# Differential attention's score products: three products of the halves, the third over 64 rows of the array

## The chip, the core and the metric

The kernel runs on one core of a Trainium2 chip. A core has five engines with an instruction stream of their own: TensorE (PE in the profile, its weight loads are PEld), VectorE (DVE), ScalarE (ACT), GpSimd (POOL) and SyncE (SP), which issues most of the DMAs. TensorE multiplies a stationary operand, loaded into its array by a weight load, with a moving operand that streams through, and adds into PSUM. The metric is the time of one execution on the device in microseconds (us), lower is better.

## The reference

One layer of a hybrid encoder, with 2048 tokens and 1024 features, in float32: a combined input projection, then a differential attention and a state-space branch (S5) with a gated linear unit, a gated merge and an output projection. The change touches the attention alone, and in it the scores `s`:

```python
def diff_attention(q, k, v, lam, rel_table, subln_gain, lam_init):
    ...
        s = jnp.einsum('bqhsd,bkhsd->bhsqk', q_blk, k).astype(jnp.float32) * scale
        bias = rel_table[t5_relative_bucket(k_pos[None, :] - q_pos[:, None])]
        ...
        s = jnp.where(allowed, s + bias, -jnp.inf)
        p = jax.nn.softmax(s, axis=-1)
        attn = p[:, :, 0] - lam * p[:, :, 1]
        return jnp.einsum('bhqk,bkhd->bqhd', attn.astype(v.dtype), v)
```

There are 4 heads, each with two sub-heads (index `s`) of 64 features; a sub-head has its own scores and softmax, and the two softmaxes are combined before they meet the values.

## The kernel before

**Numbers in halves.** TensorE works here on operands in a rounded float32 format (fp32r). To keep accuracy, q and k are split by `hilo` into a high half (rounded) and a low half (the rest). In the dense projections `split3` (L37 to L42) makes three matmuls of each product: high with high (L40), high with low (L41), low with high (L42). For the scores, `qk_norm` writes both halves of q and k to DRAM (`QS`, `KS`: sub-head s, half l, feature f, token t).

**Operands of the scores.** `Heads.head` (L480) loads for each head and sub-head a tile `K` of 128 rows: rows 0 to 63 hold the high half of the 64 features, rows 64 to 127 the low half, and 2048 columns are the tokens. `Heads.load_q` (L494) loads, for 256 queries, a tile `Q` in two versions: version 0 has the high half above the low half (L501), version 1 the low half above the high half (L502, L503). One matmul of 128 rows with version 0 thus makes high·high + low·low, one with version 1 makes high·low + low·high: two matmuls of 128 rows make four products.

**Attention.** `attention` (L514) walks over units: a head, a pair j of query blocks and one of its two blocks b, 64 units in all. A unit with n = 2j + b + 1 key blocks of 128 has its n blocks cut by `chunks` into pieces of at most 512 columns. `softmax` (L522) does for each of the two sub-heads, one after the other: per piece a PSUM tile `ps_s` out of a ring of three (`RINGS["S"]`), two matmuls (L535 and L536), one pass of VectorE that copies the scores to `e` and takes their minimum (L538, or L541 for the last piece, which adds the bias and mask); then the minimum over pieces (L546) and the exponential on ScalarE (L548). After both sub-heads VectorE combines the two (`cf` L554, `e` L558). `transposes` (L563) of a unit is recorded one unit later, `pv` (the product with the values, L572) two units later, `subln` four units later.

**Who sets the order.** The program is recorded under a scheduler that simulates the engines and sets the order of the instructions of each engine by it. In the attention stage (about 985 to 1517 us) TensorE's stream holds, beside the scores (L535, L536), the transposes (L567), the value products (L575) and the output transposes (L602), also matmuls of later phases (L40 to L42: the gated linear unit `ps_g`, the state-space projection `ps_p`, the first part of the tail `ps_a`) which the scheduler has put in between. An engine runs its stream in that order.

Of the kernel before, what the change touches and what calls it, by code (L numbers as in the profile page):

```python
# [6 lines left out]
F32 = mybir.dt.float32  # L7
F32R = mybir.dt.float32r
I32 = mybir.dt.int32
AF = mybir.ActivationFunctionType  # L10
ALU = mybir.AluOpType
AX = mybir.AxisListType
# [4 lines left out]
T = 2048  # L17
# [4 lines left out]
def f(ap):  # L22

    return ap.bitcast(F32)
# [7 lines left out]
RINGS = {"S": 3, "T": 2, "F": 2, "e0": 3, "e1": 2, "at": 8}  # L32
# [69 lines left out]
def phase1(tc, k, I, mid):  # L102

    nc = tc.nc
    with ExitStack() as es:
# [14 lines left out]
        BUFS = {"x": 4, "s": 2, "q": 2, "t": 2, "n": 2, "o": 2, "v": 2}  # L120
        W = {}

# [3 lines left out]
        def load_w(g, eng=None):  # L126

            W[g] = []
            for i in range(4):
                if i % 2 == 0:  # L130
                    wh, wl = (k.wp.tile([128, 4, 256], F32R, tag="wl", bufs=4, name="w") for _ in range(2))
                    W[g].append((wh, wl))
                raw = k.wp.tile([128, 2, 256], F32, tag="wraw", bufs=3, name="wraw")
# [30 lines left out]
        def wk(g, kk):  # L164
            return [w[:, kk % 4] for w in W[g][kk // 4]]

# [288 lines left out]
def chunks(n):  # L455

    m = (n + 3) // 4
    q, r = divmod(n, m)
    out, at = [], 0
    for i in range(m):  # L460
        w = q + (1 if i < r else 0)
        out.append((at, w))
        at += w
    return out


class Heads:
# [13 lines left out]
    def head(self, h):  # L481
        nc, k = self.nc, self.k
        self.nb = self.tile([128, 512], F32, "nb", h)
        nc.sync.dma_start(self.nb, k.NB[h])
        self.K, self.V = [], []
        for s in range(2):
            t = self.tile([128, T], F32R, "K", 2 * h + s)
            nc.sync.dma_start(f(t), f(k.KS[h][s]).rearrange("l f t -> (l f) t"))
            self.K.append(t)
        for i in range(2):  # L490
            t = self.tile([128, 8, 128], F32, "V", 2 * h + i)
            nc.sync.dma_start(t, k.VS[h][:, 8 * i:8 * i + 8])
            self.V.append(t)

    def load_q(self, h, j):
        nc, k = self.nc, self.k
        q = self.tile([128, 2, 2, 256], F32R, "Q", self.n)
        self.n += 1
        ts = slice(256 * j, 256 * j + 256)
        src = f(k.QS[h])  # L500
        nc.sync.dma_start(f(q[:, 0]), src[:, :, :, ts].rearrange("s l f t -> (l f) s t"))  # L501
        nc.sync.dma_start(f(q[0:64, 1]), src[:, 1, :, ts].rearrange("s f t -> f s t"))  # L502
        nc.sync.dma_start(f(q[64:128, 1]), src[:, 0, :, ts].rearrange("s f t -> f s t"))  # L503
        self.q[h, j] = q


# [4 lines left out]
def attention(tc, k, es, heads):  # L511
    nc = tc.nc
    pool = lambda name, **kw: es.enter_context(tc.tile_pool(name=name, bufs=1, reuse_waits="tile", **kw))
    pS = k.pS  # L514
    ap, sp = pool("ap"), pool("asm")
# [6 lines left out]
    def softmax(h, j, b, Q, Kt, nb):  # L522

        n = 2 * j + b + 1
        ch = chunks(n)
        m = len(ch)
        e, sums = [], []
        for s in range(2):
            mc = sp.tile([128, 4], F32, tag="mc", bufs=4, name="mc")
            et = ap.tile([128, T], F32, tag=f"e{s}", bufs=RINGS[f"e{s}"], name="e")[:, :128 * n]  # L530
            for i, (at, w) in enumerate(ch):
                W = 128 * w
                ps = pS.tile([128, 512], F32, tag="S", bufs=RINGS["S"], name="ps_s")[:, :W]
                ks = slice(128 * at, 128 * at + W)
                nc.tensor.matmul(ps, Q[:, 0, s, 128 * b:128 * b + 128], Kt[s][:, ks], start=True, stop=False)  # L535
                nc.tensor.matmul(ps, Q[:, 1, s, 128 * b:128 * b + 128], Kt[s][:, ks], start=False, stop=True)  # L536
                if i < m - 1:
                    nc.vector.tensor_scalar(out=et[:, ks], in0=ps, scalar1=0.0, scalar2=3e38, op0=ALU.add, op1=ALU.min,  # L538
                                            accum_out=mc[:, i:i + 1])
                else:  # L540
                    nc.vector.tensor_tensor_reduce(out=et[:, ks], in0=ps, in1=nb[:, 512 - W:], scale=1.0, scalar=3e38,  # L541
                                                   op0=ALU.add, op1=ALU.min, accum_out=mc[:, i:i + 1])
            mm = mc[:, 0:1]
            if m > 1:
                mm = sp.tile([128, 1], F32, tag="mm", bufs=4, name="mm")
                nc.vector.tensor_reduce(out=mm, in_=mc[:, 0:m], axis=AX.X, op=ALU.min)  # L546
            su = sp.tile([128, 1], F32, tag=f"su{s}", bufs=4, name="su")
            nc.scalar.activation(out=et, in_=et, func=AF.Exp, bias=mm, scale=-1.0, accum_out=su)  # L548
            e.append(et)
            sums.append(su)  # L550
        rs = sp.tile([128, 1], F32, tag="rs", bufs=3, name="rs")
        nc.vector.reciprocal(out=rs, in_=sums[1])
        cf = sp.tile([128, 1], F32, tag="cf", bufs=3, name="cf")
        nc.vector.scalar_tensor_tensor(out=cf, in0=sums[0], scalar=k.neglam, in1=rs, op0=ALU.mult, op1=ALU.mult)  # L554
        if b == 0:
            st["s2"] = sp.tile([128, 2], F32, tag="s2", bufs=3, name="s2")
        nc.gpsimd.tensor_tensor(out=st["s2"][:, b:b + 1], in0=sums[0], in1=sums[0], op=ALU.mult)
        nc.vector.scalar_tensor_tensor(out=e[0], in0=e[1], scalar=cf, in1=e[0], op0=ALU.mult, op1=ALU.add)  # L558
        return e[0]
# [49 lines left out]
    for u, (h, j, b) in enumerate(units):  # L609
        if u and u % (2 * NPAIR) == 0:  # L610
            heads.head(h)
        if b == 0:
            if (h, j) not in heads.q:
                heads.load_q(h, j)
            Q = heads.q.pop((h, j))
            pair = {}
        n = 2 * j + b + 1
        e = softmax(h, j, b, Q, heads.K, heads.nb)
        pair["s2"] = st["s2"]
        AT = []  # L620
        queue.append((u + 1, lambda n=n, e=e, AT=AT: transposes(n, e, AT)))
        queue.append((u + 2, lambda n=n, b=b, AT=AT, V=heads.V, pair=pair: pv(n, b, AT, V, pair)))
        if b == 1:
            queue.append((u + 4, lambda h=h, j=j, pair=pair: subln(h, j, pair)))
        while queue and min(queue, key=lambda x: x[0])[0] <= u:
            i = min(range(len(queue)), key=lambda i: queue[i][0])
            queue.pop(i)[1]()
# [606 lines left out]
```

## Time and profile before

| what | us |
|---|---|
| time before, median of 3 runs (1772.15 to 1774.92) | 1773.14 |
| the profiled execution's own time | 1772.99 |
| its span, first to last instruction | 1771.2 |
| VectorE busy in the span | 1032.2 |
| ScalarE busy in the span | 699.7 |
| GpSimd busy in the span | 285.8 |

The span and the execution's own time differ by 1.8 us. Busy time is a union of the instructions' times; the ends of matmuls are modelled, and consecutive matmuls overlap in it. So the pace of TensorE is read from the starts of consecutive matmuls, not from their durations. In a timeline a row gives the start, the time, the engine, the line, the operation, its operands (rows*columns of the weights, then the moving operand), how many instructions are merged in the row (x), and in brackets an idle time before it with what ended it.

### The profile page before, as it was taken

The page shows a single profiled execution, that of the slowest core. Times are in us where ns is not written, and L with a number is a line of the kernel's source. Part 1 is how long each engine was busy: PE and PEld are TensorE (multiplying, and loading weights), DVE is VectorE, ACT ScalarE, POOL GpSimd, SP SyncE. Part 2 cuts the span into 40 slices and gives each one's busy share as a digit, 9 for nine tenths or more (in the row PEclk, how much of TensorE's full clock was granted, in tenths as well). Part 3 has the DMA queues.
Part 4 walks back from the last instruction along what each step waited for, and adds up shares of the span by engine and source line. Part 5 has one row for each costly group of instructions (what it writes and reads, how often), then busy time and mean ns, then how long its engine had stood idle before and what let it go on. Part 6 is the DMA issues. An engine that isn't in the chain of part 4 may idle for free.

```text
span 1771.2 us, 24819 instructions
## 1 busy us (share of the span) xinstructions
PE 1691.9 (96%) x8720; PEld 1426.8 (81%) x8720; DVE 1032.2 (58%) x2564; ACT 699.7 (40%) x1426; POOL 285.8 (16%) x428
## 2 busy tenths in 40 slices
PE   7877999999999999999999789999999989999999
PEld 6776988888878788888888668878888879888887
DVE  7533345545734359999644587687677668643331
ACT  4533232324312243331144577675555466511100
POOL 3421000000260000000023335552111032100000
PEclk9888999999999999999999899999999999999999
DMA  5333233424343433323465764753754534654532
GB/s 166 94 92 97 67 107 78 114 76 117 103 127 121 130 119 115 110 95 100 131 203 190 237 202 144 230 169 110 221 173 127 160 103 131 196 162 148 149 101 83
DMA packets 225405, 239.05 MB, mean 135 GB/s; under 512 B 56032, under 2 KB 166016, under 8 KB 224256
## 3 DMA queue, kind: packets, MB, share of 16 engines
q1 hardware_dynamic: 182656, 210.19, 39.1%
q10 hardware_dynamic: 42624, 27.27, 5.4%
q8 instruction: 69, 1.13, 0.3%
q14 instruction: 56, 0.46, 0.1%
HBM read 146.44 MB, written 90.96 MB: 134 GB/s over the span
## 4 chain that ended last, share of the span: by engine, by line
PE 70%; DMA 13%; DVE 7%; ACT 3%; POOL 3%; issue 3%; SPq 1%; ACTq 0%; POOLq 0%; DVEq 0%
PE ps_p L40 9%; PE ps_p L41 9%; PE ps_p L42 9%; PE ps_o L575 5%; PE ps_o L40 3%; PE ps_o L42 3%; PE ps_o L41 3%; PE ps_s L536 2%; PE ps_s L535 2%; PE ps_qk L40 2%; PE ps_qk L41 2%; PE ps_qk L42 2%; PE ps_t L567 2%; DMA xs<-xT 2%; PE ps_u L42 1%
## 5 line engine op out<-in xcount | busy, mean ns | idle before, releaser
L42 PE MATMUL ps_p<-hh,w 128*128 128x512 f32 x768 | 300.3, 391 | 0.0
L40 PE MATMUL ps_p<-hh,w 128*128 128x512 f32 x768 | 300.2, 391 | 0.0
L41 PE MATMUL ps_p<-hl,w 128*128 128x512 f32 x768 | 300.1, 391 | 0.0
L41 PEld LDWEIGHTS ps_p<-hl,w 128*128 128x128 f32 x768 | 144.2, 188 | 30.1 <-issue 0.7
L42 PEld LDWEIGHTS ps_p<-hh,w 128*128 128x128 f32 x768 | 144.3, 188 | 29.5 <-issue 0.4
L40 PEld LDWEIGHTS ps_p<-hh,w 128*128 128x128 f32 x768 | 144.3, 188 | 29.0 <-issue 0.5
L548 ACT ACTIVATE e<-e,mm 128x640 f32<-128x640 f32 (+11 forms) x96 | 136.2, 1419 | 60.5 <-DVE mm L546 59.6
L575 PE MATMUL ps_o<-V,at 128*128 128x128 f32 x1088 | 149.9, 278 | 2.9 <-ACT sq L581 2.2
L575 PEld LDWEIGHTS ps_o<-V,at 128*128 128x128 f32 x1088 | 143.0, 194 | 9.7 <-ACT sq L581 2.8
L535 PE MATMUL ps_s<-K,Q 128*128 128x512 f32 (+3 forms) x320 | 129.5, 408 | 10.4 <-DMA Q<-Q 5.9
L538 DVE TENSOR_SCALAR_CACHE_REDUCE e<-ps_s 128x512 f32<-128x512 f32 (+1 forms) x192 | 120.4, 641 | 27.6 <-PE ps_s L536 26.5
L40 PE MATMUL ps_qk<-hh,w 128*128 128x512 f32 x256 | 102.5, 400 | 15.6 <-ACT hh L183 8.4
L536 PE MATMUL ps_s<-K,Q 128*128 128x512 f32 (+3 forms) x320 | 115.7, 365 | 1.2 <-DMA Q<-Q 1.1
L344 DVE TENSOR_TENSOR z<-ps_p,E 128x512 f32<-128x512 f32 x96 | 66.1, 688 | 75.2 <-PE ps_p L42 74.3
L41 PE MATMUL ps_qk<-hl,w 128*128 128x512 f32 x256 | 102.3, 400 | 4.2 <-DVE hl L184 4.2
L42 PE MATMUL ps_qk<-hh,w 128*128 128x512 f32 x256 | 101.4, 396 | 0.0
L350 ACT ACTIVATE z<-z,hmb 128x512 f32<-128x512 f32 x64 | 46.2, 723 | 124.3 <-DVE z L344 111.8
L567 PE MATMUL ps_t<-ident,e 128*128 128x128 f32 x544 | 84.7, 273 | 9.1 <-DVE e L558 3.8
L558 DVE SCALAR_TENSOR_TENSOR e<-e,cf 128x128 f32<-128x128 f32 (+7 forms) x64 | 90.1, 1407 | 1.2
L256 PE MATMUL ps_v<-w,hh 128*128 128x256 f32 x256 | 75.7, 298 | 10.2 <-ACT w L139 6.8
L569 ACT COPY at<-ps_t 128x512 f32<-128x512 f32 (+3 forms) x160 | 78.8, 520 | 16.7 <-PE ps_t L567 16.5
L567 PEld LDWEIGHTS ps_t<-ident,e 128*128 128x128 f32 x544 | 65.7, 141 | 22.0 <-ACT at L569 6.0
(346 smaller groups left out, 3691.8 us busy)
## 6 DMA issues: line engine op xcount, KB each, us to landing
wraw<-win ACTq DMA_DIRECT2D x80, 256.0 KB
TM<-z SPq DMA_DIRECT2D x32, 512.0 KB
u<-US SPq DMA_DIRECT2D x64, 128.0 KB
K<-K SPq DMA_DIRECT2D x8, 1024.0 KB
Q<-Q SPq DMA_DIRECT2D x32, 256.0 KB
Q<-Q SPq DMA_DIRECT2D x64, 128.0 KB
t<-TM SPq DMA_DIRECT2D x32, 256.0 KB
MS<-t SPq DMA_DIRECT2D x32, 256.0 KB
```

Of the source, the lines that this page charges most:

```text
L40: nc.tensor.matmul(out, wh, xh, start=start, stop=False)
L41: nc.tensor.matmul(out, wh, xl, start=False, stop=False)
L42: nc.tensor.matmul(out, wl, xh, start=False, stop=stop)
L256: nc.tensor.matmul(ps, xh, wh, start=kk == 0, stop=False)
L535: nc.tensor.matmul(ps, Q[:, 0, s, 128 * b:128 * b + 128], Kt[s][:, ks], start=True, stop=False)
L536: nc.tensor.matmul(ps, Q[:, 1, s, 128 * b:128 * b + 128], Kt[s][:, ks], start=False, stop=True)
L538: nc.vector.tensor_scalar(out=et[:, ks], in0=ps, scalar1=0.0, scalar2=3e38, op0=ALU.add, op1=ALU.min, accum_out=mc[:, i:i + 1])
L548: nc.scalar.activation(out=et, in_=et, func=AF.Exp, bias=mm, scale=-1.0, accum_out=su)
L558: nc.vector.scalar_tensor_tensor(out=e[0], in0=e[1], scalar=cf, in1=e[0], op0=ALU.mult, op1=ALU.add)
L567: nc.tensor.transpose(pt[:, x], e[:, o:o + 128], k.ident)
L569: nc.scalar.copy(AT[g][:, :w], pt[:, :w])
L575: nc.tensor.matmul(po, AT[x // 4][:, x % 4], Vt[x // 8][:, x % 8], start=x == 0, stop=x == n - 1)
```

## The change

The scores are made of three products in place of four (low·low is left out). The tile `K` of sub-head 0 has the high half in rows 0 to 63 and the low half in rows 64 to 127, that of sub-head 1 the reverse. Version 0 of `Q` now holds q's high half in both row halves, so that one matmul of 128 rows makes high·high + high·low (q's high half with k's two halves). Version 1 holds q's low half once, sub-head 0's in rows 0 to 63 and sub-head 1's in rows 64 to 127; with k's high half, which lies in the same rows, it makes the third product in a matmul of 64 rows. The two sub-heads are now computed piece by piece together: two matmuls of 128 rows, then the two of 64 rows, in different rows of the array, then VectorE's two passes. The minimum and exponential come after all pieces.

```diff
         for s in range(2):
             t = self.tile([128, T], F32R, "K", 2 * h + s)
-            nc.sync.dma_start(f(t), f(k.KS[h][s]).rearrange("l f t -> (l f) t"))
+
+            for l in range(2):
+                nc.sync.dma_start(f(t[64 * (l ^ s):64 * (l ^ s) + 64]), f(k.KS[h][s][l]))
             self.K.append(t)
...
-        nc.sync.dma_start(f(q[:, 0]), src[:, :, :, ts].rearrange("s l f t -> (l f) s t"))
-        nc.sync.dma_start(f(q[0:64, 1]), src[:, 1, :, ts].rearrange("s f t -> f s t"))
-        nc.sync.dma_start(f(q[64:128, 1]), src[:, 0, :, ts].rearrange("s f t -> f s t"))
+
+        for i in range(2):
+            r = slice(64 * i, 64 * i + 64)
+            nc.sync.dma_start(f(q[r, 0]), src[:, 0, :, ts].rearrange("s f t -> f s t"))
+            nc.sync.dma_start(f(q[r, 1, 0]), src[i, 1, :, ts])
...
-        e, sums = [], []
+        mc = [sp.tile([128, 4], F32, tag="mc", bufs=4, name="mc") for _ in range(2)]
+        e = [ap.tile([128, T], F32, tag=f"e{s}", bufs=RINGS[f"e{s}"], name="e")[:, :128 * n] for s in range(2)]
+        sums = []
+        bs = slice(128 * b, 128 * b + 128)
+        for i, (at, w) in enumerate(ch):
+            W = 128 * w
+            ks = slice(128 * at, 128 * at + W)
+            ps = [pS.tile([128, 512], F32, tag="S", bufs=RINGS["S"], name="ps_s")[:, :W] for _ in range(2)]
+            for s in range(2):
+                nc.tensor.matmul(ps[s], Q[:, 0, s, bs], Kt[s][:, ks], start=True, stop=False)
+            for s in range(2):
+                r = slice(64 * s, 64 * s + 64)
+                nc.tensor.matmul(ps[s], Q[r, 1, 0, bs], Kt[s][r, ks], start=False, stop=True)
+            for s in range(2):
+                if i < m - 1:
+                    nc.vector.tensor_scalar(out=e[s][:, ks], in0=ps[s], scalar1=0.0, scalar2=3e38, op0=ALU.add,
+                                            op1=ALU.min, accum_out=mc[s][:, i:i + 1])
+                else:
+                    nc.vector.tensor_tensor_reduce(out=e[s][:, ks], in0=ps[s], in1=nb[:, 512 - W:], scale=1.0, scalar=3e38,
+                                                   op0=ALU.add, op1=ALU.min, accum_out=mc[s][:, i:i + 1])
         for s in range(2):
-            mc = sp.tile([128, 4], F32, tag="mc", bufs=4, name="mc")
-            et = ap.tile([128, T], F32, tag=f"e{s}", bufs=RINGS[f"e{s}"], name="e")[:, :128 * n]
-            for i, (at, w) in enumerate(ch):
-                W = 128 * w
-                ps = pS.tile([128, 512], F32, tag="S", bufs=RINGS["S"], name="ps_s")[:, :W]
-                ks = slice(128 * at, 128 * at + W)
-                nc.tensor.matmul(ps, Q[:, 0, s, 128 * b:128 * b + 128], Kt[s][:, ks], start=True, stop=False)
-                nc.tensor.matmul(ps, Q[:, 1, s, 128 * b:128 * b + 128], Kt[s][:, ks], start=False, stop=True)
...
-            nc.scalar.activation(out=et, in_=et, func=AF.Exp, bias=mm, scale=-1.0, accum_out=su)
-            e.append(et)
+            nc.scalar.activation(out=e[s], in_=e[s], func=AF.Exp, bias=mm, scale=-1.0, accum_out=su)
```

In the changed file the two score matmuls stand in lines L540 (128 rows) and L543 (64 rows), the transposes in L575, the value products in L583. The scheduler makes a new order of it. Two places of TensorE's stream show how, both in head 0. In the rows the numbers are buffer numbers (K_8646 is sub-head 0's tile of k; sub-head 1's is K_8648 before and K_8649 after), and the last column is the size of the output.

The first place is a unit of eleven key blocks, cut in pieces of 512, 384 and 384 columns. TensorE's stream before, from the unit's first piece of sub-head 0:

```order
L535 MATMUL ps_s_9138<-K_8646,Q_9062 128x512
L536 MATMUL ps_s_9138<-K_8646,Q_9062 128x512
L40 MATMUL ps_g_13744<-gh0_13721,gw_hi_13703 128x512
L40 MATMUL ps_g_13764<-gh0_13721,gw_hi_13703 128x512
L535 MATMUL ps_s_9142<-K_8646,Q_9062 128x384
L536 MATMUL ps_s_9142<-K_8646,Q_9062 128x384
L575 MATMUL ps_o_9109<-V_8650,at_9054 128x128 x4
L535 MATMUL ps_s_9146<-K_8646,Q_9062 128x384
L536 MATMUL ps_s_9146<-K_8646,Q_9062 128x384
```

The same unit after, from the same piece:

```order
L540 MATMUL ps_s_9147<-K_8646,Q_9068 128x512
L543 MATMUL ps_s_9147<-K_8646,Q_9068 128x512
L583 MATMUL ps_o_9116<-V_8652,at_9060 128x128 x4
L540 MATMUL ps_s_9148<-K_8649,Q_9068 128x512
L543 MATMUL ps_s_9148<-K_8649,Q_9068 128x512
L583 MATMUL ps_o_9116<-V_8652,at_9066 128x128 x3
L40 MATMUL ps_g_13784<-gh0_13761,gw_hi_13743 128x512
L40 MATMUL ps_g_13804<-gh0_13761,gw_hi_13743 128x512
L540 MATMUL ps_s_9155<-K_8646,Q_9068 128x384
L543 MATMUL ps_s_9155<-K_8646,Q_9068 128x384
L540 MATMUL ps_s_9156<-K_8649,Q_9068 128x384
L543 MATMUL ps_s_9156<-K_8649,Q_9068 128x384
```

The two sub-heads now alternate, but the order written in the code (two of 128 rows, then two of 64) is not the order of the stream: each matmul of 64 rows stands right behind the matmul of 128 rows of its own tile, alone, and is followed by one of 128 rows.

The second place is the next larger unit (thirteen key blocks: 512, 384, 384, 384 columns). Before, from its first piece of sub-head 0:

```order
L535 MATMUL ps_s_9407<-K_8646,Q_9401 128x512
L567 MATMUL ps_t_9388<-ident_61,e_9231 128x128 x4
L536 MATMUL ps_s_9407<-K_8646,Q_9401 128x512
L41 MATMUL ps_g_13764<-gl3_13740,gw_hi_13703 128x512
L42 MATMUL ps_g_13764<-gh3_13739,gw_lo_13702 128x512
L535 MATMUL ps_s_9411<-K_8646,Q_9401 128x384
L536 MATMUL ps_s_9411<-K_8646,Q_9401 128x384
```

After, from the first piece of sub-head 1 on:

```order
L540 MATMUL ps_s_9419<-K_8649,Q_9409 128x512
L543 MATMUL ps_s_9419<-K_8649,Q_9409 128x512
L583 MATMUL ps_o_9375<-V_8654,at_9313 128x128 x2
L575 MATMUL ps_t_9389<-ident_61,e_9240 128x128 x4
L540 MATMUL ps_s_9426<-K_8646,Q_9409 128x384
L540 MATMUL ps_s_9427<-K_8649,Q_9409 128x384
L543 MATMUL ps_s_9426<-K_8646,Q_9409 128x384
L543 MATMUL ps_s_9427<-K_8649,Q_9409 128x384
L575 MATMUL ps_t_9396<-ident_61,e_9240 128x128 x4
```

Here the second piece has the two matmuls of 64 rows next to each other, as the code has it. Counted over the whole of TensorE's stream after: 320 matmuls of 128 rows (L540) and 320 of 64 rows (L543) stand where 640 of 128 rows stood; 38 of the 64-row ones stand in 19 pairs, the other 282 alone, so they make 301 stretches, each with instructions of 128 rows on both sides. The number of TensorE's matmuls is the same in both programs.

More of the change, by code (lines that the diff above doesn't have):

```diff
@@ L526, in softmax @@
         m = len(ch)
-        e, sums = [], []
-        for s in range(2):
-            mc = sp.tile([128, 4], F32, tag="mc", bufs=4, name="mc")
-            et = ap.tile([128, T], F32, tag=f"e{s}", bufs=RINGS[f"e{s}"], name="e")[:, :128 * n]
-            for i, (at, w) in enumerate(ch):
-                W = 128 * w
-                ps = pS.tile([128, 512], F32, tag="S", bufs=RINGS["S"], name="ps_s")[:, :W]
-                ks = slice(128 * at, 128 * at + W)
[L535 to L543, printed above, removed]
+        mc = [sp.tile([128, 4], F32, tag="mc", bufs=4, name="mc") for _ in range(2)]
@@ L544, in softmax @@
+        for s in range(2):
+            mm = mc[s][:, 0:1]
             if m > 1:
                 mm = sp.tile([128, 1], F32, tag="mm", bufs=4, name="mm")
-                nc.vector.tensor_reduce(out=mm, in_=mc[:, 0:m], axis=AX.X, op=ALU.min)
+                nc.vector.tensor_reduce(out=mm, in_=mc[s][:, 0:m], axis=AX.X, op=ALU.min)
             su = sp.tile([128, 1], F32, tag=f"su{s}", bufs=4, name="su")
-            nc.scalar.activation(out=et, in_=et, func=AF.Exp, bias=mm, scale=-1.0, accum_out=su)
```

## The prediction

> **What bounds the kernel now.** First the page: share of each engine, the chain that ended last, and the scores among the costliest groups.
>
> ```profile
> span 1771.2 us, 24819 instructions
> PE 1691.9 (96%) x8720; PEld 1426.8 (81%) x8720; DVE 1032.2 (58%) x2564; ACT 699.7 (40%) x1426; POOL 285.8 (16%) x428
> PE 70%; DMA 13%; DVE 7%; ACT 3%; POOL 3%; issue 3%; SPq 1%; ACTq 0%; POOLq 0%; DVEq 0%
> L535 PE MATMUL ps_s<-K,Q 128*128 128x512 f32 (+3 forms) x320 | 129.5, 408 | 10.4 <-DMA Q<-Q 5.9
> L536 PE MATMUL ps_s<-K,Q 128*128 128x512 f32 (+3 forms) x320 | 115.7, 365 | 1.2 <-DMA Q<-Q 1.1
> ```
>
> TensorE is busy for 96% of the span and is 70% of the chain. The average hides stages, so next the busy time by stretches: the first 60 us of attention, its rest, and what comes behind it.
>
> ```profile
> 985.00:1045.00 60.00, 42.49 (x244) 34.83 (x243) 44.33 (x131) 43.37 (x111) 23.83 (x40) 0.91 0.79 233
> 1045.00:1517.00 472.00, 453.85 (x2801) 396.74 (x2800) 346.38 (x960) 290.01 (x639) 133.81 (x228) 0.99 0.51 156
> 1517.00:1771.00 254.00, 249.31 (x1096) 202.16 (x1094) 92.17 (x142) 36.36 (x74) 6.51 (x16) 1.00 0.46 139
> ```
>
> Columns: length, then busy time of TensorE, its weight loads, VectorE, ScalarE, GpSimd, then the granted clock and the share of the DMA engines. From 1045 to 1517 TensorE is busy 453.85 of 472 us at a clock of 0.99, VectorE only 346.38. Later phases' matmuls fill the holes of attention, and behind it TensorE works on at 249.31 of 254. So **TensorE's stream is the bound from 1045 us to the end**: whatever time it gains or loses per matmul in attention reaches the end, except for what its idle time takes up, 60 − 42.49 = 17.5 us in the first 60 us and 472 − 453.85 = 18.2 us in the rest. What it waits for there, from the list of waits for 985 to 1517 us:
>
> ```profile
> PE ps_s L535 <- DMA Q<-Q: 5.9, 1, 5.9
> PE ps_t L567 <- DVE e L558: 3.8, 3, 2.6
> PE ps_t L567 <- ACT at L569: 3.5, 3, 1.9
> PE ps_s L535 <- DVE e L538: 3.3, 5, 1.0
> ```
>
> **Pace of TensorE's matmuls.** From the timeline of TensorE in mid-attention, where nothing is waited for:
>
> ```profile
> 1207.51 0.40 PE L536 MATMUL ps_s<-K,Q 128*128 128x512 f32 x1
> 1207.74 0.33 PE L535 MATMUL ps_s<-K,Q 128*128 128x384 f32 x1
> 1207.91 0.34 PE L536 MATMUL ps_s<-K,Q 128*128 128x384 f32 x1
> 1208.09 0.39 PE L40 MATMUL ps_p<-os,pw_hi 128*128 128x512 f32 x1
> 1208.32 0.40 PE L41 MATMUL ps_p<-os,pw_hi 128*128 128x512 f32 x1
> ```
>
> From start to start: 0.23 us for 512 columns, 0.17 for 384, whatever the line. The two matmuls of 128 rows cost a PSUM tile of 512 columns 0.46 us.
>
> **What the change is about, in the best case.** The third product alone needs half the rows. If the two sub-heads' 64-row matmuls ran beside each other, one of four streams would go in each of the 160 pairs of pieces. The piece sizes follow from `chunks`: for the 16 blocks of a head 20 of 512 columns, 17 of 384, 2 of 256 and 1 of 128, or 17,408 columns, times 4 heads 69,632, at 0.23 us per 512 columns 31.3 us. But only 19 of the 160 pairs stand next to each other in the new stream (counted above, with an example at the second place): the scheduler puts each 64-row matmul behind its own 128-row one, as I read it because of the ring of three PSUM tiles, in which the other sub-head's tile is not free yet. Those 19 hold 7,680 columns, 3.4 us at most. A 64-row matmul that stands alone streams as many columns as before and saves nothing.
>
> **What the change adds: the array changes its shape.** In attention no matmul of the old kernel has fewer than 128 rows. The nearest rows in this trace are the bias matmuls of 32 rows (L437, L438), which stand among 128-row matmuls of a projection. Twice TensorE goes into 32 rows and out again in the first passage, and once in the second:
>
> ```profile
> 871.87 0.39 PE L41 MATMUL ps_p<-hl,w 128*128 128x512 f32 x1
> 872.10 0.39 PE L42 MATMUL ps_p<-hh,w 128*128 128x512 f32 x1
> 872.32 0.39 PE L40 MATMUL ps_p<-hh,w 128*128 128x512 f32 x1
> 872.64 0.60 PE L437 MATMUL ps_b<-ohr,tbh 32*128 32x384 f32 x2
> 873.18 0.50 PE L41 MATMUL ps_p<-hl,w 128*128 128x512 f32 x1
> 873.51 0.40 PE L42 MATMUL ps_p<-hh,w 128*128 128x512 f32 x1
> 873.84 0.61 PE L438 MATMUL ps_b<-ohr,tbl 32*128 32x384 f32 x2
> 874.38 0.50 PE L40 MATMUL ps_p<-hh,w 128*128 128x512 f32 x1
> 874.72 0.40 PE L41 MATMUL ps_p<-hl,w 128*128 128x512 f32 x1
> ...
> 879.30 0.39 PE L40 MATMUL ps_p<-hh,w 128*128 128x512 f32 x1
> 879.61 0.43 PE L437 MATMUL ps_b<-ohr,tbh 32*128 32x384 f32 x1
> 879.89 0.33 PE L438 MATMUL ps_b<-ohr,tbl 32*128 32x384 f32 x1
> 880.06 0.33 PE L437 MATMUL ps_b<-ohr,tbh 32*128 32x384 f32 x1
> 880.24 0.33 PE L438 MATMUL ps_b<-ohr,tbl 32*128 32x384 f32 x1
> 880.50 0.50 PE L41 MATMUL ps_p<-hl,w 128*128 128x512 f32 x1
> 880.84 0.40 PE L42 MATMUL ps_p<-hh,w 128*128 128x512 f32 x1
> ```
>
> First passage, 872.32 to 874.72: 2.40 us for eight starts. Their plain pace is 4 × 0.23 (512 columns) + 4 × 0.17 (384) = 1.60, so 0.80 us for four changes of shape. Second, 879.30 to 880.84: 1.54 us against 2 × 0.23 + 4 × 0.17 = 1.14, so 0.40 for two. **One change costs 0.20 us**, in six of six. It falls in two halves: the start after the change comes about 0.09 late (872.64 − 872.32 = 0.32 for 0.23), and the one after that about 0.10 late (873.51 − 873.18 = 0.33 for 0.23). Between matmuls of one shape (879.89, 880.06, 880.24) there is nothing. The rows of the weight loads say why:
>
> ```profile
> 872.10 0.19 PEld L40 LDWEIGHTS ps_p<-hh,w 128*128 128x128 f32 x1
> 872.64 0.29 PEld L437 LDWEIGHTS ps_b<-ohr,tbh 32*128 32x128 f32 x2 [0.35 <-issue]
> ```
>
> L40's weights go in at 872.10, 0.22 us ahead of its matmul (872.32), while the matmul before still runs. [...]
>
> **The sum.** The 301 stretches of 64 rows have a change on each side: 602 changes × 0.20 = **+120.4 us** of TensorE's stream. [...] A gain per change is excluded: a matmul of 64 rows streams the same columns. The 19 adjacent pairs: between 0 (L437 and L438, all in rows 0 to 31, keep the full 0.17 each) and −3.4; I take −2. [...] No row here shows two row groups side by side.
>
> Then the idle time. A slower TensorE waits less for the others, whose work stays the same: from 0 to −(17.5 + 18.2) = −35.7. The first 60 us wait mostly for loads and a first unit's latency (5.9 us for Q alone) and should keep theirs; the 18.2 us behind are waits for VectorE and ScalarE, which at 346.38 and 290.01 of 472 have room. I take **−18**.
>
> At nothing I cost the loads. Q's three issues become four of three quarters of the bytes, K's one becomes two halves; Q's own issues take this on SyncE's queue:
>
> ```profile
> L501 SPq DMA_DIRECT2D Q<-Q x32: 362/374/1103, 981.5 to 1482.2; - x32
> L502 SPq DMA_DIRECT2D Q<-Q x32: 579/586/1726, 983.4 to 1482.6; - x32
> ```
>
> That is at most 0.6 us more per Q load, 32 times in 532 us, on a queue that runs ahead of TensorE; without that cover each late load would cost its lateness, 19 us in all at worst. VectorE's and ScalarE's instructions keep their number and size; a sub-head's exponential now comes after both sub-heads' pieces, hidden by the later phases' matmuls and by the transposes being recorded one unit later. If that cover failed, the price is a wait like those of L567 above, 1 us each. As both are within the idle bound, they go into the range.
>
> 120.4 − 2 − 18 = +100.4. On the profiled execution's 1772.99 us (span 1771.2 and 1.8 around it, 0.15 below the median of the runs) that is **1873 us**, 5.7% slower.
>
> **Rivals.**
> 1. [...] Chance 0.09.
> 2. No price, not slower: 64 rows count as a masked 128-row matmul, no change of shape at all. Then the lone ones pace as before and the pairs give 0 to −3.4: **1770 to 1773**. It decides from a price of 3.4 / 602 = 0.006 us per change downwards. Against it are the six changes above. Chance 0.05, most of it within the bound of no change.
> 3. The change does what it says, in all pairs: −31.3, **1742**. It needs all 160 pairs adjacent; the stream has 19. Chance 0.02.
> 4. Dearer: no idle time taken up, and new waits because VectorE's two passes now come bunched and one PSUM tile of three stays blocked longer: +120 and again the 17.5 us of a badly filled start, **1910**. Chance 0.06.
>
> The forecast's case, 1845 to 1900 (idle time from −35.7 to about 0, changes at 0.19 to 0.21), has 0.78.
>
> **How the numbers follow.** The likeliest case gives 1873. The upper end of the range takes idle time at 0 and half of rival 4's new waits (1773 + 120 + 9, about 1903); the lower one reaches to rival 1 (1818), which leaves out rivals 2 and 3 and part of 4. A measurement of this kernel tells about 0.2% (3.5 us) from no change. Faster by more: rival 3 and a little of rival 2, 0.03. Within: most of rival 2, 0.04. Slower: the rest, 0.93.
>
> **What would show it.** In the changed profile a start-to-start time from L540 to L543 of 0.23 + 0.09 for 512 columns, and about 0.34 or more from L543 to what follows; L543's weight loads starting with their matmul, not 0.2 us ahead; TensorE's share of the attention stage's idle smaller; the stage some 100 us longer with the same number of matmuls, and the stretches before 985 and after attention unchanged. In an adjacent pair the second L543 starting at once behind the first would show side-by-side work. Wrong would be: L540 to L543 at 0.23 with loads ahead (rival 2), a clock below 0.9 in attention (a cause that I don't count, as it is 0.99 now), or a longer stage with the extra time as idle behind DMA or VectorE (rival 4).

## The result and the profile after

The changed kernel takes **1879.03 us** (median of 4 runs, 1871.65 to 1881.24) against 1772.89 us (the kernel before, median of 4 runs): ratio 1.0589, 95% interval [1.0557, 1.0622], 106 us slower. The profiled execution took 1880.91 us, its span 1878.8. From the page of after: the engines, the chain that ended last, and the scores (L540 with 128 rows, L543 with 64) with the latter's weight loads.

```profile
span 1878.8 us, 24846 instructions
PE 1806.7 (96%) x8720; PEld 1434.9 (76%) x8720; DVE 1050.7 (56%) x2564; ACT 704.2 (37%) x1426; POOL 286.4 (15%) x428
PE 80%; DMA 8%; DVE 4%; POOL 2%; ACT 2%; issue 2%; SPq 1%; ACTq 0%; POOLq 0%; DVEq 0%
L543 PE MATMUL ps_s<-K,Q 64*128 64x384 f32 (+3 forms) x320 | 143.1, 475 | 0.0
L540 PE MATMUL ps_s<-K,Q 128*128 128x512 f32 (+3 forms) x320 | 139.4, 445 | 1.0 <-DVE mc L549 0.4
L543 PEld LDWEIGHTS ps_s<-K,Q 64*128 64x128 f32 x320 | 56.7, 188 | 72.8 <-issue 69.4
```

The number of matmuls is as before (8720), and TensorE's busy time is 114.8 us longer. The last row is the one to look at: the loads of 64 rows stand 72.8 us behind an idle load path, and nearly all of it (69.4) is "issue", a wait for nothing that the profile names.

The same stretches as before the change, from the view by windows (length, busy TensorE, weight loads, VectorE, ScalarE, GpSimd, clock, DMA share and rate):

```profile
985.00:1045.00 60.00, 40.32 (x138) 28.67 (x136) 28.88 (x76) 28.24 (x71) 15.64 (x26) 0.65 0.60 174
1045.00:1624.00 579.00, 571.38 (x2899) 410.02 (x2900) 380.05 (x1013) 309.56 (x679) 141.53 (x242) 0.99 0.44 129
1624.00:1878.00 254.00, 250.60 (x1110) 204.00 (x1108) 92.96 (x144) 37.06 (x74) 6.14 (x16) 1.00 0.46 139
```

What comes behind attention has kept its 254 us. All of the loss lies in the attention stage: 579 us in place of 472 behind its first 60 us, with only 7.6 us of TensorE idle in place of 18.2. The first 60 us differ too: 138 matmuls in place of 244 are done in them, at a granted clock of 0.65 in place of 0.91, so a part of the 107 us is work that they left undone.

The price is seen in TensorE's timeline, between later matmuls:

```profile
1201.13 0.40 PE L42 MATMUL ps_g<-gh,gw_lo 128*128 128x512 f32 x1
1201.37 0.40 PE L540 MATMUL ps_s<-K,Q 128*128 128x512 f32 x1
1201.69 0.49 PE L543 MATMUL ps_s<-K,Q 64*128 64x512 f32 x1
1202.12 0.73 PE L40 MATMUL ps_g<-gh,gw_hi 128*128 128x512 f32 x2
1202.68 0.40 PE L540 MATMUL ps_s<-K,Q 128*128 128x512 f32 x1
1203.01 0.50 PE L543 MATMUL ps_s<-K,Q 64*128 64x512 f32 x1
1203.44 0.49 PE L540 MATMUL ps_s<-K,Q 128*128 128x512 f32 x1
1203.86 0.50 PE L543 MATMUL ps_s<-K,Q 64*128 64x512 f32 x1
1204.29 1.16 PE L583 MATMUL ps_o<-V,at 128*128 128x128 f32 x8
```

A 512-column matmul follows its predecessor by 0.23 us at plain pace. Here L543 starts 0.32 us behind L540 (1201.37 to 1201.69), what follows it 0.43 behind it, and two tiles of this kind in a row stand 0.85 apart (1203.01 to 1203.86), where the tile's two matmuls took 0.46 before: about 0.39 more for two changes. It is the same throughout: behind 1060 us 136 lone 64-row matmuls of 512 columns have a next start 0.427 us later at the median (0.421 to 0.432 for nine in ten). The weight loads of the same place:

```profile
1202.45 0.19 PEld L540 LDWEIGHTS ps_s<-K,Q 128*128 128x128 f32 x1
1203.01 0.18 PEld L543 LDWEIGHTS ps_s<-K,Q 64*128 64x128 f32 x1 [0.37 <-issue]
1203.44 0.19 PEld L540 LDWEIGHTS ps_s<-K,Q 128*128 128x128 f32 x1 [0.25 <-issue]
```

Without a change of shape L540's load goes ahead of its matmul (1202.45 for 1202.68). With one on each side, loads start together with their matmuls (1203.01, 1203.44).

### The profile page after: what moved, and what is told of

It reads as the page before. It is cut to its first block, busy times and chain, and to the rows that moved or that the text cites. A ratio compares the mean times of both kernels' runs of the same rounds, so it can differ in the third digit from the quotient of the medians.

```text
span 1878.8 us, 24846 instructions
## 1 busy us (share of the span) xinstructions
PE 1806.7 (96%) x8720; PEld 1434.9 (76%) x8720; DVE 1050.7 (56%) x2564; ACT 704.2 (37%) x1426; POOL 286.4 (15%) x428
## 4 chain that ended last, share of the span: by engine, by line
PE 80%; DMA 8%; DVE 4%; POOL 2%; ACT 2%; issue 2%; SPq 1%; ACTq 0%; POOLq 0%; DVEq 0%
PE ps_p L40 9%; PE ps_p L41 9%; PE ps_p L42 9%; PE ps_o L583 7%; PE ps_s L543 6%; PE ps_s L540 4%; PE ps_t L575 3%; PE ps_o L40 3%; PE ps_o L41 3%; PE ps_o L42 3%; PE ps_qk L41 2%; PE ps_qk L42 2%; PE ps_qk L40 2%; DMA xs<-xT 2%; PE ps_a L42 2%
## 5 line engine op out<-in xcount | busy, mean ns | idle before, releaser
L583 PE MATMUL ps_o<-V,at 128*128 128x128 f32 x1088 | 157.2, 286 | 0.1
L583 PEld LDWEIGHTS ps_o<-V,at 128*128 128x128 f32 x1088 | 139.2, 196 | 17.3 <-issue 13.2
L543 PE MATMUL ps_s<-K,Q 64*128 64x384 f32 (+3 forms) x320 | 143.1, 475 | 0.0
L540 PE MATMUL ps_s<-K,Q 128*128 128x512 f32 (+3 forms) x320 | 139.4, 445 | 1.0 <-DVE mc L549 0.4
L543 PEld LDWEIGHTS ps_s<-K,Q 64*128 64x128 f32 x320 | 56.7, 188 | 72.8 <-issue 69.4
L549 DVE CUSTOM_DVE_ANT_0 e<-ps_s,nb 128x384 f32<-128x384 f32 (+3 forms) x128 | 69.4, 555 | 57.7 <-PE ps_s L543 42.8
L575 PE MATMUL ps_t<-ident,e 128*128 128x128 f32 x544 | 87.0, 282 | 3.2 <-DVE e L566 2.8
```

Source lines behind the costliest of these rows:

```text
L540: nc.tensor.matmul(ps[s], Q[:, 0, s, bs], Kt[s][:, ks], start=True, stop=False)
L543: nc.tensor.matmul(ps[s], Q[r, 1, 0, bs], Kt[s][r, ks], start=False, stop=True)
L549: nc.vector.tensor_tensor_reduce(out=e[s][:, ks], in0=ps[s], in1=nb[:, 512 - W:], scale=1.0, scalar=3e38, op0=ALU.add, op1=ALU.min, accum_ ...
L575: nc.tensor.transpose(pt[:, x], e[:, o:o + 128], k.ident)
L583: nc.tensor.matmul(po, AT[x // 4][:, x % 4], Vt[x // 8][:, x % 8], start=x == 0, stop=x == n - 1)
```

## The experiments

All ratios are to the kernel before, run on the same chip beside them. The scheduler makes a new order for each of these kernels. The diffs show the lines that matter; `...` marks lines left out.

**Order alone.** The changed loops, but the loads (left out here) and four products of before:

```diff
...
             for s in range(2):
-                r = slice(64 * s, 64 * s + 64)
-                nc.tensor.matmul(ps[s], Q[r, 1, 0, bs], Kt[s][r, ks], start=False, stop=True)
+                nc.tensor.matmul(ps[s], Q[:, 1, s, bs], Kt[s][:, ks], start=False, stop=True)
```

> The changed loop order (both sub-heads piece by piece) with the loads and the four products of before, all matmuls of 128 rows. Theory A (each change between 64 and 128 rows costs TensorE about 0.20 us): no change of shape is left in attention, so 1773 us, at most some 20 us off for a different start of the stage. Theory B (the new order, bunched VectorE passes and waits for PSUM cost the time): it keeps the cost, 1860 us or more.

Measured: 1775.19 us (10 runs) against 1775.58, ratio 1.0004 [0.9988, 1.0019]. The interleaved loops and the bunched VectorE passes cost nothing; theory B falls.

**Rows alone.** The loops of before, with the changed loads (left out here) and the third product over 64 rows:

```diff
...
-                nc.tensor.matmul(ps, Q[:, 1, s, 128 * b:128 * b + 128], Kt[s][:, ks], start=False, stop=True)
+                r = slice(64 * s, 64 * s + 64)
+                nc.tensor.matmul(ps, Q[r, 1, 0, 128 * b:128 * b + 128], Kt[s][r, ks], start=False, stop=True)
```

> The loop order of before (one sub-head after the other) with the changed loads and the third product over 64 rows. In its stream 318 of the 64-row matmuls stand alone and two stand together, 319 stretches. Theory A: 638 changes x 0.20 = 128 us, less some 20 us of idle time taken up: 1875 to 1890 us. Theory B: 1773 us, since the order is that of before.

Measured: 1877.19 us, ratio 1.0581 [1.0546, 1.0617]. The whole loss comes with the rows and their loads. Its windows:

```profile
985.00:1045.00 60.00, 40.41 (x137) 29.14 (x137) 27.60 (x73) 27.56 (x67) 15.25 (x26) 0.67 0.63 180
1045.00:1622.00 577.00, 576.71 (x2927) 412.21 (x2927) 370.16 (x1020) 312.76 (x685) 141.03 (x242) 1.00 0.44 130
```

From 1045 us on TensorE has no idle time left (0.3 us). The poor first 60 us (137 matmuls at a clock of 0.67) are here as in the changed kernel. The order-only kernel did 264 in them:

```profile
985.00:1045.00 60.00, 45.88 (x264) 39.43 (x265) 46.91 (x142) 44.40 (x113) 26.75 (x44) 0.89 0.81 240
```

So the start does not hang on the loop order. What this kernel shares with the changed one are the rows and the loads, and the prediction had priced the loads at nothing; they are tested on their own below.

**Pairs kept together, and their control.** One PSUM tile of twice the width (two times 512 columns) for the two sub-heads of a piece, in a ring of two; the scores then hold the room of four old tiles in place of three, and the fourth is taken from the transposes:

```diff
-RINGS = {"S": 3, "T": 2, "F": 2, "e0": 3, "e1": 2, "at": 8}
+RINGS = {"S": 2, "T": 1, "F": 2, "e0": 3, "e1": 2, "at": 8}
...
-            ps = [pS.tile([128, 512], F32, tag="S", bufs=RINGS["S"], name="ps_s")[:, :W] for _ in range(2)]
+            pp = pS.tile([128, 2, 512], F32, tag="S", bufs=RINGS["S"], name="ps_s")
+            ps = [pp[:, s, :W] for s in range(2)]
...
```

> The changed kernel, with one PSUM tile of two banks for the two sub-heads of a piece (ring of two, the transposes' ring cut from two to one), so that 158 of 160 pairs of 64-row matmuls stand next to each other. Theory A, with pairs that run beside each other: against e4_pairs_128 +320 x 0.20 = 64 less 31 of saved streams, so about 25 to 35 us slower than it and some 70 us faster than the changed kernel (about 1800 to 1810). If adjacent ones don't run side by side: 55 to 65 us slower than e4_pairs_128. If only the order counts (B): equal to e4_pairs_128.

> The control of e3_pairs: the same PSUM tiles and rings and the same loop order, but four products with matmuls of 128 rows and the loads of before. All theories: what the smaller ring for the transposes and the double tiles cost by themselves, 1770 to 1800 us.

Measured: the pairs 1900.32 us (ratio 1.0697 [1.0669, 1.0725]), the control 1877.7 (1.0576 [1.0554, 1.0598]). The difference, 22.6 us, is close to the 25 to 35 expected of pairs that run beside each other and far from the 55 to 65 of pairs that don't. But both were expected faster, the pairs by 90 to 100 us and the control by 78 to 108: the rings themselves cost 102 us. And the two differ in more than the rows: the pairs' kernel has the changed loads, the control those of before (k in halves alone costs 16.6 us, below), and behind 1060 us TensorE idles for 74 and 85 us in them, in which a part of any cost can hide. So the times alone don't settle whether pairs run beside each other; the timeline does. Two pieces in a row of the pairs:

```profile
1208.30 0.71 PE L541 MATMUL ps_s<-K,Q 128*128 128x512 f32 x2
1208.95 0.49 PE L544 MATMUL ps_s<-K,Q 64*128 64x512 f32 x2
1209.37 0.73 PE L541 MATMUL ps_s<-K,Q 128*128 128x512 f32 x2
1210.04 0.49 PE L544 MATMUL ps_s<-K,Q 64*128 64x512 f32 x2
```

The two 64-row matmuls together take 0.42 us up to the next start (1208.95 to 1209.37), no more than a single one in the changed kernel (0.43). They do run side by side. The kernel with k in one load (below) is the counter-test: there both sub-heads' 64-row matmuls stand in the same rows, and some of them are adjacent too:

```profile
1272.40 0.73 PE L540 MATMUL ps_s<-K,Q 64*128 64x512 f32 x2
1273.06 0.49 PE L538 MATMUL ps_s<-K,Q 128*128 128x512 f32 x1
```

Here the two take 0.66 us up to the next start. Being adjacent was not enough: the two that ran side by side (0.42 us) stood in different rows, the two that did not (0.66) in the same ones.

But in the pairs' kernel a piece of both sub-heads takes 1.07 us (1208.30 to 1209.37), where four 128-row matmuls take 0.92: with one stretch of 64 rows per pair the two changes (0.40) outweigh the saved stream (0.23) even when every pair is adjacent.

**What made the control slow.** The kernel before with one PSUM tile for the transposes:

```diff
-RINGS = {"S": 3, "T": 2, "F": 2, "e0": 3, "e1": 2, "at": 8}
+RINGS = {"S": 3, "T": 1, "F": 2, "e0": 3, "e1": 2, "at": 8}
```

> The kernel before with the ring of the transposes' PSUM tiles cut from two to one, nothing else. If this cut is what made e4_pairs_128 slow (102 us; its TensorE waits for ScalarE's copies of the transposes, 30.9 us in 25 waits): most of those 102 us, 1840 to 1880. If the double score tiles did it: near 1776.

Measured: 1844.28 us, ratio 1.0383 [1.0344, 1.0421], 69 of the control's 102 us. From the lists of TensorE's waits in the attention stage (total, times, longest), the control's row first, then this kernel's:

```profile
PE ps_t L572 <- ACT at L574: 30.9, 25, 3.5
```

```profile
PE ps_t L567 <- ACT at L569: 21.8, 26, 2.1
```

With one tile a group of transposes can wait for ScalarE's copy of the last, 26 times here against 3 before (3.5 us). These 21.8 us are only a part of the 69; the rest was not taken apart. Nor was what the control's other 33 us are (the double tiles held for two sub-heads, perhaps, by the control's new waits for VectorE).

**Loads: k in one DMA.** The changed kernel with each tile of k loaded as before; both sub-heads' 64-row matmuls then stand in rows 0 to 63:

```diff
-            for l in range(2):
-                nc.sync.dma_start(f(t[64 * (l ^ s):64 * (l ^ s) + 64]), f(k.KS[h][s][l]))
+            nc.sync.dma_start(f(t), f(k.KS[h][s]).rearrange("l f t -> (l f) t"))
...
-            nc.sync.dma_start(f(q[r, 1, 0]), src[i, 1, :, ts])
+        nc.sync.dma_start(f(q[0:64, 1]), src[:, 1, :, ts].rearrange("s f t -> f s t"))
...
-                r = slice(64 * s, 64 * s + 64)
-                nc.tensor.matmul(ps[s], Q[r, 1, 0, bs], Kt[s][r, ks], start=False, stop=True)
+                nc.tensor.matmul(ps[s], Q[0:64, 1, s, bs], Kt[s][0:64, ks], start=False, stop=True)
```

> The changed kernel with k loaded as before (one DMA over 128 rows for each tile, high half above low half), so that the 64-row matmuls of both sub-heads stand in rows 0 to 63 (297 stretches, pairs can't run beside each other). Theory L (the loads of k in halves of 64 rows arrive late, so that the stage starts some 15 us late and then at a low clock): the first score matmul at about 990 us as before, not 1005, and the time 10 to 18 us below the changed kernel's 1879, less 3 of lost pairs: 1864 to 1872. If the loads are hidden: 1879 to 1882.

Measured: 1856.02 us, ratio 1.0458 [1.0434, 1.0483], 23 us below the changed kernel and more than the 10 to 18 expected. The first score matmul starts at 992.7 us, not 1005.2. Q is still loaded in parts of 64 rows here.

**Loads: k split, nothing else.** The kernel before with its k in two DMAs:

```diff
-            nc.sync.dma_start(f(t), f(k.KS[h][s]).rearrange("l f t -> (l f) t"))
+            for l in range(2):
+                nc.sync.dma_start(f(t[64 * l:64 * l + 64]), f(k.KS[h][s][l]))
```

> The kernel before with one edit: each tile of k is loaded in two DMAs of 64 rows, its halves where they were. Theory L: the stage starts some 15 us late and the time is 8 to 18 us longer, 1781 to 1791. If the loads are hidden: 1773.

Measured: 1792.58 us, ratio 1.0094 [1.0078, 1.0111], 16.6 us slower. No instruction of another engine was edited, but the scheduler's order of TensorE's stream differs from 985 us on, so the cost is that of the split loads and of the order made for them. The first score matmul starts at 1002.3 us in place of 990.3. Windows of the loads (965 to 985 us) and the start of the stage (985 to 1060), the kernel before first, then this one:

```profile
965.00:985.00 20.00, 20.00 (x100) 16.89 (x99) 7.66 (x11) 7.37 (x15) 6.14 (x7) 1.00 0.87 302
985.00:1060.00 75.00, 56.20 (x327) 46.02 (x326) 56.07 (x161) 54.40 (x133) 31.26 (x53) 0.93 0.71 212
```

```profile
965.00:985.00 20.00, 20.00 (x102) 16.96 (x101) 6.97 (x10) 7.12 (x14) 5.57 (x6) 1.00 0.95 242
985.00:1060.00 75.00, 54.54 (x257) 45.50 (x256) 47.63 (x140) 46.81 (x117) 29.50 (x46) 0.75 0.76 215
```

The DMA engines are busier (0.95 for 0.87) and move less (242 GB/s for 302). In the DMA records of about this stretch a packet of 8 KB, one row of k, takes 309 ns at the median before and 571 in this kernel, and the 256 packets of the first head's k start over 18.4 us in place of 7.1 (in the changed kernel, whose k is split too, 620 ns and 19.1 us). TensorE then waits for the small loads of the state-space branch behind k in the same queue. This shows in the list of what waits for whom from 975 to 1060 us (total, times, longest):

```profile
ACT th L865 <- DMA tm<-KD: 15.1, 3, 10.5
PE ps_y L40 <- ACT uh L865: 6.3, 2, 4.6
```

ScalarE waits 15.1 us for those loads (`tm`) and TensorE in turn for ScalarE. The granted clock is 0.75 for 0.93, and 257 matmuls are done in place of 327 in these 75 us. TensorE's idle time is nearly that of before (20.5 for 18.8 us), so most of what is lost here is lost at a lower clock. In the clock's records it falls to half in two waits, one of 4.6 us (at 989.7) and one of 3.2 (at 999.9), and the second time it stays there for 27.3 us; before it fell in a wait of 5.9 us, for 6.8. What held it down so long was not taken apart.

**One sub-head only.** The order and k load of before; sub-head 0 has the third product over 64 rows, sub-head 1 its four products (q's load, left out here, is put in five parts to fit):

```diff
...
+                r = slice(0, 128 if s else 64)
-                nc.tensor.matmul(ps, Q[:, 1, s, 128 * b:128 * b + 128], Kt[s][:, ks], start=False, stop=True)
+                nc.tensor.matmul(ps, Q[r, 1, s, 128 * b:128 * b + 128], Kt[s][r, ks], start=False, stop=True)
```

> The order of before, k in one load; only sub-head 0 has three products with the third over 64 rows, sub-head 1 keeps its four products in 128 rows. 160 stretches of 64 rows, 320 changes. Theory A: 320 x 0.20 = 64 us less 10 to 18 of idle time, 1819 to 1827; half of what e2_rows_only gave beyond its start. If the cost came from the loads or from a fixed effect of 64-row work: near 1773 or near 1877.

Measured: 1810.35 us, ratio 1.0188 [1.0168, 1.0208]: 34 us for 320 changes, where theory A expected 46 to 54 over before. Between none and all, as a price per change demands, but less than half of the 80 us of 594 changes with k in one load: the first changes are paid out of idle time, as the rests of the next table bear out.

**One price for all.** To test the 0.20 us per change I counted, for each profiled execution, TensorE's matmuls from 1060 us to the last score matmul. Each counts with its plain pace from the trace of before (229, 172 and 117 ns for 512, 384 and 256 columns, 110 for 128), each change with 0.20 us:

| kernel | length, us | plain pace | changes | saved by pairs | rest |
|---|---|---|---|---|---|
| before | 457.3 | 425.5 | 0 | 0 | 31.8 |
| one sub-head | 490.5 | 428.0 | 276 × 0.20 = 55.2 | 0 | 7.4 |
| k in one load | 541.5 | 435.2 | 526 × 0.20 = 105.2 | 0 | 1.2 |
| rows alone | 562.3 | 445.6 | 586 × 0.20 = 117.2 | 0 | −0.5 |
| changed kernel | 566.3 | 447.8 | 558 × 0.20 = 111.6 | 3.1 | 10.0 |

The rest is all that TensorE's stream does not explain. With many changes it goes to zero: TensorE is then gapless (0.75 us idle with k in one load), and 0.20 us per change fits. The table tests price and plain pace together: 1% of the pace (4.4 of 435.2 us) would move the price by 0.008 us. The changed kernel's 10.0 is less clean: 7.6 of it are idle in the profile, in six waits, the longest for ScalarE (3.4 and 2.3 us). K split alone has a rest of 41.2 here against 31.8, so about half of its cost falls behind the start; whether the later heads' loads of k cause either was not taken apart. From 985 to 1060 us, worked out in the same way, the rest is 28.7 before, 23.5 with k in one load, 39.1 with k split alone and 41.4 in the changed kernel.

## Why the prediction came out right, and where it was wrong

**Right: the bound and the price.** TensorE's stream was the bound, and a change between 128 and 64 rows costs the 0.20 us read from the six changes to 32 rows. That 64 rows cost what 32 do was an estimate, as no row of before has 64; the runs showed it, with 0.39 us for two changes. The signs named ahead came: L543 0.32 us behind L540, 0.43 up to what follows, its loads starting with it, the tail's 254 us unchanged. So both halves of the price are there: a start about 0.09 us late, and the next start about 0.11 late where the weight load starts together with its own matmul (1203.01 and 1203.44, as L437's at 872.64 before), not 0.23 us ahead (1202.45 for 1202.68). Why the first start is late no run shows. The 602 changes were the likeliest case's one large term, and rivals 1 to 3 fall with it: no half price, no free shape, no gain. The 1818 us of rival 1, the range's lower end, takes 0.10 us per change; no run shows such a change, and the runs showed 0.20. Rival 4's badly filled start came, but not by its cause: with the new loop order alone the time is that of before (1775.19 us).

**Right: few pairs, and they run side by side.** The term −2 lies at −3.6 over both windows: an adjacent pair starts as one, which saves the whole of the second stream (the 19 pairs hold 7,808 columns in the trace, not 7,680). In the changed kernel's timeline:

```profile
1110.24 0.71 PE L540 MATMUL ps_s<-K,Q 128*128 128x512 f32 x2
1110.88 0.50 PE L543 MATMUL ps_s<-K,Q 64*128 64x512 f32 x2
1111.32 0.50 PE L41 MATMUL ps_g<-gl,gw_hi 128*128 128x512 f32 x1
```

Both L543 together take 0.44 us up to the next start; in the records their starts lie 3 to 4 ns apart, against 335 to 345 ns where two of 512 columns stand in the same rows (k in one load).

**Wrong in size: "I take −18" of idle time.** With k in one load, the changed kernel with the least of the new loads, the rest falls from 31.8 to 1.2 and at the start from 28.7 to 23.5, together −35.8. I had counted the idle time that the profile shows behind 1045 us (18.2) and kept the start's. Behind 1060 us the profile shows 16.9 us idle before and 0.75 here, so only about 16 of these 30.6 us were idle to be seen. The others are times by which matmuls started later than the plain pace without an idle row. Waits hidden under a matmul's modelled end and the error of the single figures taken for the pace are the likely parts; they were not taken apart.

**Wrong: "At nothing I cost the loads".** The step looked at SyncE's issue times and bytes and named 19 us as the worst. The transfers themselves became slower: k in parts of 64 rows moves at nearly half the pace per packet (571 ns for 8 KB in place of 309). Alone this costs 16.6 us; in the changed kernel, by the rests above, (41.4 + 10.0) − (23.5 + 1.2) = 26.7, part of it through the low clock of the first 60 us (0.65), a sign of being wrong that the prediction had named as a cause that it doesn't count. What made the packets slower was not shown: each split made two DMAs of 64 rows out of one of 128, so no run here tells the fewer rows from the greater number of DMAs.

The two errors cancel for the most part: 120.4 − 3.6 − 35.8 + 26.7 = 107.7, and the span grew by 107.6 us. That this closes is no further test, since the rests are what the counts leave over. The idle term was 18 us too small and the loads 27 us too cheap; that the forecast of 1873 us lies only 6 us off is luck in these two terms, not in the large one.

## What to carry to other kernels

In this kernel using fewer rows of the array saved nothing by itself: behind a lone 64-row matmul of 512 columns the next starts 0.427 us later, behind one of 128 rows at plain pace 0.23. The gain was only in matmuls that ran beside each other, in different rows (0.42 to 0.44 us for the two up to the next start), and every switch into and out of that shape cost a start about 0.09 us late and a weight load not ahead of its matmul, about 0.11 more. Count the switches in the order that the scheduler really made, not in the code: here 602 at 0.20 us each against 19 streams of at most 0.23. Even one pair between two switches loses (0.40 against 0.23); by these numbers two pairs of 512 columns would just pay (0.46), an estimate that no run here tests. And where an operand's layout is cut so that its load covers half of the partitions, price the transfer itself, not its bytes or issue time: here a packet of 8 KB took 571 ns in place of 309.

## What the runs showed of the hardware that was not expected

- Loads of k in two DMAs over 64 rows took almost twice as long per 8 KB packet as in one over 128 (571 against 309 ns), at the same total of bytes.
- The badly filled start was paid twice: with k split alone TensorE idled only 1.7 us more from 985 to 1060 us, but the clock granted there fell from 0.93 to 0.75.
- One PSUM tile fewer for the transposes cost this kernel 69 us, more than k's split loads alone (16.6) and a good part of what 602 changes of shape did.
